# A two-layer hybrid network on one core: both scan directions in one instruction, and attention scores of all keys in one PSUM tile

## The chip, the cores and the metric

The kernel runs on one core of a Trainium2 chip. Each core has a matrix engine (TensorE, PE in the profile, with its weight loads as PEld), three elementwise engines (VectorE = DVE, ScalarE = ACT, GpSimd = POOL), a sync engine that issues the DMAs (SP), and DMA queues. Every engine works through its own instructions in order and waits for the others by semaphores. Matmul results land in PSUM, which has eight banks of 512 F32 columns in 128 partitions each. The metric is device time in microseconds (us); the kernel before takes 4089.88 us, the median of three runs.

## The reference, cut to what matters

Two layers run over 1280 tokens (256 of context, 1024 latent) of width 1024. Layer 0 computes differential attention beside a bidirectional RWKV-7 scan and adds both through one output projection; then comes an MLP. Layer 1 has two other scans and an MLP; the change does not touch it. The two mixers of layer 0:

```python
def _diff_softmax_mix(q, k, v, lam):          # 4 heads, two score maps each
    s = einsum('bhmqd,bhmkd->bhmqk', q, k) * (A_QK_DIM ** -0.5)
    p = softmax(s, axis=-1)
    w = p[:, :, 0] - lam * p[:, :, 1]
    return einsum('bhqk,bhkd->bhqd', w, v)    # then an rmsnorm over each head's 128 columns

def step(S, inp):                             # RWKV-7, 8 heads of 64, once forward, once backward
    r_t, w_t, k_t, v_t, kk_t, a_t = inp
    sa = einsum('bhvk,bhk->bhv', S, kk_t)
    S = (S * w_t - sa * (kk_t * a_t) + v_t * k_t)
    return S, einsum('bhvk,bhk->bhv', S, r_t)
# y = y_forward + flip(y_backward), then a group norm, a bonus term and a gate
```

Context queries see the 256 context keys; latent queries see all 1280.

## The kernel before, in words

Features lie on the partitions and tokens along the free axis, so one tile is 128 features by 1280 tokens. Most matrix products are written as three fp32r matmuls over a high and a low half of each operand (helper lines L82 to L84 or L945 and L946; the splitting subtractions have line L94 and the casts L90 and L92).

Layer 0 goes through three stages that this change touches.

**Pairs.** For each of the four pairs of RWKV heads, `pair` (from L406) takes the projected r, k, v and makes the decay sums `rw_cs` for both directions (a scan on DVE, L426), kk, kk·a and the new k, and writes them in token order to DRAM: `rw_win` holds four slots of a window of 128 tokens, `rw_cs` the decay sums.

**Projections beside the scan.** `at.by_group` projects q, k, v of the attention, with rope, and stores them to DRAM in halves. While it is emitted, the scan's calls to `pump()` advance it by `RATE[0]` generator steps each (class `Pump`), for the first three sweeps (`FIRST`).

**Attention beside the scan.** The scan has ten sweeps of two windows each, one window per direction. A sweep is `prep` for both directions (`prep_dir`: load the window, exponentials `rE`, `rEi` of the decay sums, products `rkr` on DVE at L543 and L544 and `rbk` on POOL at L547, the 128-by-128 score blocks at L555 with their masks at L559, an inverse of a unit triangular matrix in `inverse`, and `values`) and two chunks of `step`, which carry the state `S` (update at L702 and L703). Each direction has its own instructions and its own bank (`si` or `sj` in the inverse, `ss` in the step). When both directions of a window are done, `post` normalizes and stores it (L754 to L772); that is so after the second sweep and after the last four. The pump now advances `at.heads` by `RATE[1]`: for each head and each pair of query blocks, `scores` makes 128 queries by 1280 keys in three pieces of 256, 512 and 512 columns, each in a bank `mm` (two of them), takes a maximum (L948) and an exponential with its sum (L949) of each piece. `factors` works out what each piece is to be scaled by, `mix` scales and subtracts (L977 on POOL, L978 on DVE), transposes the weights (L987), splits them (`a_wh`, `a_wl`) and multiplies by v in three matmuls per 128 keys into `po`.

When the scan is through, the output projection `wout0` starts on the RWKV outputs `o`, with the banks `sp`, `si`, `sj` (`TAIL_TAGS`); what is left of the attention runs beside it.

Within each engine the order of the program is set by a scheduler from the order in which the code is written, the dependencies and its own estimates of time; so the generator steps and the banks set what stands next to what.

## Time and profile before

| | |
|---|---|
| three runs, us | 4087.19, 4089.88, 4095.32 |
| the profiled execution, us | 4086.29, of which 4084.5 from the first to the last instruction (span) |
| mean granted clock of TensorE | 0.942 of full speed |
| PE busy | 3821.4 us (94%), 31232 matmuls |
| DVE busy | 2121.8 us (52%) |
| ACT, POOL busy | 1237.3 us (30%), 1448.5 us (35%) |
| DMA | 392.40 MB, mean 96 GB/s |

Busy time is the union of an engine's instructions. For PE the ends of matmuls are modelled, so neighbouring records overlap, and a slower granted clock makes the same work count as more busy time. Shares over the whole span hide the stages. Those that the change touches lie at 60 to 388 us (pairs), 388 to 742 us (projections beside the scan) and 742 to 1425 us (attention beside the scan), and the end of the attention reaches to about 1500 us. A row of a group view has the line, engine, operation and tiles, then busy time and the mean of one, then how long the engine was idle before them and what released it.

### The profile page before, as it was taken

The numbers are of one execution on the slowest core, as the hardware profiler recorded it, in microseconds if no ns is written. First come the engines' busy times: TensorE is split into PE (matmuls) and PEld (weight loads), VectorE is DVE, ScalarE is ACT, GpSimd is POOL, SyncE is SP. The second block draws the span as 40 slices with busy tenths as digits, with TensorE's granted clock in tenths as the row PEclk, the third lists the DMA queues.
The fourth block names the chain that finished last, engine by engine and source line by source line (L and its number), as shares of the span: only waits on it lengthen the run. The fifth ranks groups of instructions, "written<-read, shape, count | busy, mean of one in ns | idle before, by whom it ended". The sixth has DMA issues, their size and how long they took to land. (4 is left out here: it accounts for less than half of the span.)

```text
span 4084.5 us, 75847 instructions
## 1 busy us (share of the span) xinstructions
PE 3821.4 (94%) x31232; PEld 3137.6 (77%) x31232; DVE 2121.8 (52%) x4634; ACT 1237.3 (30%) x2391; POOL 1448.5 (35%) x1386
## 2 busy tenths in 40 slices
PE   6998899889888799999999999899999889999998
PEld 4765777667666587778878888778876678999897
DVE  6233566777776666333333445447336664443445
ACT  3332323343443425111111112574633141111112
POOL 2321666323433235222122223216524353233323
PEclk9998899888887799999999999999999789999999
DMA  8356654322232522221121102122343311111111
GB/s 306 123 157 191 216 182 161 116 73 90 84 94 57 176 98 90 88 82 64 61 83 52 37 31 89 57 66 81 109 119 104 104 50 57 42 42 58 47 42 63
DMA packets 281882, 392.40 MB, mean 96 GB/s; under 512 B 54080, under 2 KB 184128, under 8 KB 278976
## 3 DMA queue, kind: packets, MB, share of 16 engines
q1 hardware_dynamic: 281536, 387.55, 29.4%
q8 instruction: 246, 4.03, 0.4%
q14 instruction: 100, 0.82, 0.1%
HBM read 295.97 MB, written 91.49 MB: 95 GB/s over the span
## 5 line engine op out<-in xcount | busy, mean ns | idle before, releaser
L82 PE MATMUL mm<-acth,whi 128*128 128x512 f32 (+1 forms) x2376 | 838.4, 354 | 15.0 <-ACT cv_t L1042 7.7
L83 PE MATMUL mm<-actl,whi 128*128 128x512 f32 (+1 forms) x2376 | 834.2, 352 | 18.3 <-DVE actl L255 11.6
L94 POOL TENSOR_TENSOR wlo<-wraw,whi 128x1024 fp32r<-128x1024 f32 (+2 forms) x267 | 557.6, 2094 | 798.1 <-ACT whi L90 795.1
L84 PE MATMUL mm<-acth,wlo 128*128 128x512 f32 (+1 forms) x2376 | 824.7, 351 | 0.0
L82 PEld LDWEIGHTS mm<-acth,whi 128*128 128x128 f32 x2376 | 455.0, 192 | 100.2 <-issue 21.1
L83 PEld LDWEIGHTS mm<-actl,whi 128*128 128x128 f32 x2376 | 455.1, 192 | 87.2 <-DVE actl L255 13.1
L84 PEld LDWEIGHTS mm<-acth,wlo 128*128 128x128 f32 x2376 | 453.4, 192 | 65.7 <-issue 8.0
L90 ACT CAST whi<-wraw 128x1024 fp32r<-128x1024 f32 (+2 forms) x267 | 242.7, 921 | 647.9 <-PE mm L83 265.6
L313 POOL TENSOR_TENSOR relu<-relu 128x256 f32<-128x256 f32 (+1 forms) x192 | 159.9, 833 | 733.3 <-ACT relu L312 731.5
L312 ACT ACTIVATE relu<-mm 128x256 f32<-128x256 f32 (+1 forms) x192 | 93.8, 489 | 819.2 <-PE mm L84 646.6
L92 DVE CAST hidh<-relu 128x256 fp32r<-128x256 f32 (+1 forms) x192 | 71.6, 373 | 450.0 <-POOL relu L313 447.8
L82 PE MATMUL sp<-hidh,whi 128*128 128x256 f32 (+1 forms) x768 | 260.6, 339 | 0.0
L83 PE MATMUL sp<-hidl,whi 128*128 128x256 f32 (+1 forms) x768 | 259.7, 338 | 0.0
L84 PE MATMUL sp<-hidh,wlo 128*128 128x256 f32 (+1 forms) x768 | 259.0, 337 | 0.0
L83 PE MATMUL ss<-hidl,whi 128*128 128x256 f32 (+1 forms) x720 | 242.3, 337 | 1.4 <-DVE hidl L94 1.4
L82 PE MATMUL ss<-hidh,whi 128*128 128x256 f32 (+1 forms) x720 | 242.5, 337 | 0.0
L84 PE MATMUL ss<-hidh,wlo 128*128 128x256 f32 (+1 forms) x720 | 241.9, 336 | 0.0
L337 DVE SCALAR_TENSOR_TENSOR x<-sp,g,x 128x512 f32<-128x512 f32 (+1 forms) x192 | 126.9, 661 | 151.9 <-PE sp L84 151.9
L337 DVE SCALAR_TENSOR_TENSOR x<-ss,g,x 128x256 f32<-128x256 f32 x180 | 119.1, 662 | 148.1 <-PE ss L84 148.1
L949 ACT ACTIVATE a_e<-mm,a_mx 128x512 f32<-128x512 f32 (+1 forms) x208 | 125.7, 605 | 178.6 <-DVE a_mx L948 170.3
L337 DVE SCALAR_TENSOR_TENSOR x<-sp,g2b,x 128x256 f32<-128x256 f32 (+1 forms) x192 | 109.5, 571 | 99.8 <-PE sp L84 98.6
L84 PEld LDWEIGHTS sp<-hidh,wlo 128*128 128x128 f32 x768 | 144.5, 188 | 20.3 <-issue 4.5
(538 smaller groups left out, 7955.6 us busy)
## 6 DMA issues: line engine op xcount, KB each, us to landing
mraw<-in_modw_dram SPq DMA_DIRECT2D x192, 256.0 KB, 3.0
wraw<-in_win_dram SPq DMA_DIRECT2D x75, 512.0 KB, 3.7
wraw<-in_wa_dram SPq DMA_DIRECT2D x64, 512.0 KB, 3.3
wraw<-in_wb_dram SPq DMA_DIRECT2D x64, 512.0 KB, 3.3
rx<-rw_win SPq DMA_DIRECT2D x20, 1024.0 KB, 6.2
x<-in_xT_dram SPq DMA_DIRECT2D x16, 640.0 KB, 8.1
hg<-h SPq DMA_DIRECT2D x32, 256.0 KB, 5.1
wraw<-in_wout_dram SPq DMA_DIRECT2D x32, 256.0 KB, 2.8
```

The source lines that it names most:

```text
L82: self.nc.tensor.matmul(out, lh, rh, start=start and i == 0, stop=False)
L83: self.nc.tensor.matmul(out, lh, rl, start=False, stop=False)
L84: self.nc.tensor.matmul(out, ll, rh, start=False, stop=stop and i == n - 1)
L90: nc.scalar.copy(out=hi, in_=src)
L92: nc.vector.tensor_copy(out=hi, in_=src)
L94: e.tensor_tensor(out=lo, in0=src, in1=hi.bitcast(F32), op=ALU.subtract)
L312: nc.scalar.activation(out=r, in_=ps, func=AF.Relu)
L313: nc.gpsimd.tensor_tensor(out=r, in0=r, in1=r, op=ALU.mult)
L337: nc.vector.scalar_tensor_tensor(out=xg, in0=ps, scalar=gate[:, m, j : j + 1], in1=xg, op0=ALU.mult, op1=ALU.add)
L949: nc.scalar.activation(out=e[:, k0 : k0 + kn], in_=ps, func=AF.Exp, bias=mx, accum_out=o["z"][:, b, m, g : g + 1])
```

## The change

Four things change, and the scheduler moves the rest.

1. `pair` multiplies the decays in once for all tokens, at the end, on tiles of 1280 columns, and writes `rw_kr` and `rw_bk` in the order in which the scan of each direction meets them; `prep` loads them as they are. `rE`, `rEi`, `rkr` and `rbk` of the sweep are gone, and the end-of-chunk decays stay in a constant tile `rw_end`.
2. Both directions go through one instruction per phase: tiles of 16 units in place of 8 in the inverse, 512 columns in place of 256 in `step`. All of the scan, and `post`, takes its PSUM from one tag `rw` with three banks.
3. `scores` puts all keys of 128 queries into one tile `at` of three banks (there is one such tile), with one maximum and one exponential over 1280 columns. The factors between pieces go, and 1/z moves to the norm at the end.
4. The weights and v stay whole F32: one F32 matmul (two passes) in place of three fp32r ones; neither is split. The pump goes at 3.7 and 0.95 steps, and the first-stage projections take turns on `mm` and `po`, one bank each.

```diff
-        wv = lambda slot, lo, hi: self.win[:, lo:hi, slot, i, :].rearrange("w p t -> p w t")
-        nc.sync.dma_start(out=wv(0, 0, P), in_=sv(kk, 0, P))
...
+            nc.scalar.activation(out=E[:, :, 1:65], in_=chunks(cs), func=AF.Exp, scale=-self.HC)
+            nc.gpsimd.tensor_copy(out=self.end[:, :, 4 * d + i : 4 * d + i + 1], in_=E[:, :, 64:65])
+            nc.scalar.activation(out=cs, in_=cs, func=AF.Exp, scale=self.HC)
+            Ei = chunks(cs)
+            for src, e, eng, to in ((kk, E[:, :, 0:64], nc.vector, 0), (kka, Ei, nc.gpsimd, (0, 1)),
+                                    (r, E[:, :, 1:65], nc.vector, 1), (kf, Ei, nc.gpsimd, (1, 0))):
+                t = tmp("rw_t")
+                for a, b in segs:
+                    c = slice(a // 64, b // 64)
+                    eng.tensor_tensor(out=chunks(t)[:, c], in0=chunks(way(src[:, a:b])), in1=e[:, c], op=ALU.mult)
+                if eng is nc.vector:
+                    nc.sync.dma_start(out=self.kr[d][:, :, to, i].rearrange("w p t -> p w t"), in_=t.rearrange("p (w t) -> p w t", t=P))
+                    continue
+                for rows, slot in zip((slice(0, 64), slice(64, P)), to):
+                    nc.sync.dma_start(out=self.bk[d][rows, i, :, slot], in_=chunks(t)[rows])
...
-        return [self.prep_dir(sw, d) for d in range(2)]
...
+        for d in range(2):
+            for c in range(2):
+                tok = slice(c * 64, c * 64 + 64)
+                ps = [n.psum(512, "rw") for _ in range(2)]
+                for i in range(4):
+                    for hh in range(2):
+                        rows = slice(64 * hh, 64 * hh + 64)
+                        nc.tensor.matmul(ps[hh][:, i * P : i * P + P], bk[d][rows, i, c], kr[d][rows, :, i, tok], start=True, stop=True)
+                sc[d, c] = []
+                for hh in range(2):
+                    s = T([P, 4, P], f"rs{hh}", 6)
+                    nc.vector.tensor_tensor(out=s, in0=ps[hh].rearrange("p (i t) -> p i t", i=4),
+                                            in1=k["scmask"].unsqueeze(1).to_broadcast([P, 4, P]), op=ALU.mult)
...
+        o["u"] = self.inverse(mb.rearrange("p d c i t -> p (d c i) t"), sc)
...
+        units = [(d, i, hh, rows) for d in range(2) for i in range(4) for hh, rows in enumerate((A, B))]
+        ps = n.psum(512, "rw")
+        for d, i, hh, rows in units:
+            nc.tensor.matmul(part(ps, d, i)[rows], kr[d][rows, 0, i, tok], S[rows, d, i], start=True, stop=True)
...
-            for (w, y), tag in zip(self.done, ("si", "sj")):
-                self.post(self.out, w, y, tag)
+            for w, d, y in self.done:
+                self.post(self.out, w, d, y, "rw")
...
-        for g, (k0, kn) in enumerate(o["groups"]):
-            ps = n.psum(kn)
...
+        ps = n.psum(1536, "at")
+        qh, ql = o["q"][m]
+        for k0 in range(0, nk, 512):
+            s = slice(k0, min(k0 + 512, nk))
+            nc.tensor.matmul(ps[:, s], qh[:, q], K[m][:, s], start=True, stop=False)
+            nc.tensor.matmul(ps[:, s], ql[:, q], K[m][:, s], start=False, stop=True)
+        mx = o["mx"][:, b, m : m + 1]
+        nc.vector.tensor_reduce(out=mx, in_=ps[:, :nk], op=ALU.max, axis=AX.X, negate=True)
+        nc.scalar.activation(out=e[:, :nk], in_=ps[:, :nk], func=AF.Exp, bias=mx, accum_out=o["z"][:, b, m : m + 1])
...
-                nc.gpsimd.tensor_scalar(out=e1[:, s], in0=e1[:, s], scalar1=f[:, b, 1, g : g + 1], scalar2=1.0, op0=ALU.mult, op1=ALU.mult)
+            nc.vector.scalar_tensor_tensor(out=e0, in0=e1, scalar=f[:, b : b + 1], in1=e0, op0=ALU.mult, op1=ALU.add)
...
-            wh, wl = tl("a_wh", F32R, 512, 2), tl("a_wl", F32R, 512, 2)
-            n.split(wh, wl, ps, "a", "v")
+            w = tl("a_w", F32, 512, 2)
+            nc.scalar.copy(out=w, in_=ps)
+            for kk in range(2):
+                nc.tensor.matmul(po, v[:, 2 * k2 + kk], w[:, kk * 256 : kk * 256 + 256], start=k2 + kk == 0, stop=kk == 1 and k2 == nk // 256 - 1)
...
-TAIL_TAGS = ("sp", "si", "sj")
+TAIL_TAGS = ("rw",)
-FIRST, RATE = 3, (2.6, 1.0)
+FIRST, RATE = 3, (3.7, 0.95)
...
-        n.banks(("mm",), mm=2, po=1, sp=1, si=1, sj=1, ss=2)
+        n.banks(("mm", "po"), mm=1, po=1, at=1, rw=3)
```

How the change moves the instructions is seen at three places. The first is DVE in the attention stage, in the middle of a sweep. Before (`rpm`, `sav`, `S` belong to a step, `rsk`, `rsr`, `id`, `itt` to the next sweep's preparation, `a_` to the attention):

```order
L680 TENSOR_TENSOR rpm<-rbv,ss 128x256
L978 SCALAR_TENSOR_TENSOR a_e_10104<-a_e_10104,a_f,a_e_10194 128x256
L680 TENSOR_TENSOR rpm<-rbv,ss 128x256
L632 COPY_PREDICATED id<-t_masks_85,si 128x16x8
L978 SCALAR_TENSOR_TENSOR a_e_10104<-a_e_10104,a_f,a_e_10194 128x512
L559 TENSOR_TENSOR rsk_12345<-sp,t_masks_85 128x256
L559 TENSOR_TENSOR rsr_12346<-sp,t_masks_85 128x256
L978 SCALAR_TENSOR_TENSOR a_e_10104<-a_e_10104,a_f,a_e_10194 128x512
L619 STREAM_TRANSPOSE itt<-id 128x256
L978 SCALAR_TENSOR_TENSOR a_e_10220<-a_e_10220,a_f,a_e_10246 128x256
L689 TENSOR_SCALAR sav_10128<-ss 64x256
L978 SCALAR_TENSOR_TENSOR a_e_10220<-a_e_10220,a_f,a_e_10246 128x512
```

And the same engine after the change, from a step on:

```order
L667 TENSOR_TENSOR rpm<-rbv,rw 128x512
L925 TENSOR_REDUCE a_mx<-at 128x1
L674 TENSOR_SCALAR sav_7979<-rw 64x512
L683 TENSOR_TENSOR S<-S,rw 128x512
L684 TENSOR_TENSOR S<-S,rw_end 128x512
L925 TENSOR_REDUCE a_mx<-at 128x1
L667 TENSOR_TENSOR rpm<-rbv,rw 128x512
L932 RECIPROCAL a_r<-a_z 128x4
L933 COPY a_rz<-a_r 128x2
L935 SCALAR_TENSOR_TENSOR a_f<-a_r,lam_n,a_z 128x2
L946 SCALAR_TENSOR_TENSOR a_e_9821<-a_e_9935,a_f,a_e_9821 128x1280
L946 SCALAR_TENSOR_TENSOR a_e_10039<-a_e_10088,a_f,a_e_10039 128x1280
```

Before, work of one direction's step lies between pieces of the other direction's preparation and of the attention; after, one step is a run of 512-column instructions, with whole maxima and whole mixes of 1280 columns between its links.

The second place is PE in the same stage. Before (`si` and `sj` are the inverse's banks, `sp` the score blocks, `ss` the step, `mm` and `po` the attention's):

```order
L630 MATMUL si<-id,iwt 32x32 x3
L987 MATMUL mm<-ident,a_e_11022 128x128
L987 MATMUL mm<-ident,a_e_10756 128x128
L987 MATMUL mm<-ident,a_e_11022 128x128
L630 MATMUL si<-id,iwt 32x32 x11
L555 MATMUL sp<-rkr,rbk 128x128 x2
L82 MATMUL po<-a_wh,avh 128x256
L555 MATMUL sp<-rkr,rbk 128x128 x2
L684 MATMUL ss<-rpm,iu 64x64 x11
L83 MATMUL po<-a_wl,avh 128x256
L84 MATMUL po<-a_wh,avl 128x256
```

And after, in the middle of an inverse:

```order
L953 MATMUL mm<-ident,a_e_12039 128x128
L953 MATMUL mm<-ident,a_e_12238 128x128
L618 MATMUL rw<-id,iwt 32x32 x64
L922 MATMUL at<-ak_10905,aqh_12312 128x512
L923 MATMUL at<-ak_10905,aql_12313 128x512
L922 MATMUL at<-ak_10905,aqh_12312 128x512
L923 MATMUL at<-ak_10905,aql_12313 128x512
L922 MATMUL at<-ak_10905,aqh_12312 128x256
L923 MATMUL at<-ak_10905,aql_12313 128x256
L957 MATMUL po<-a_w,av 128x256 x2
```

An inverse's 64 matmuls now stand in one run, followed by the six matmuls of a score tile and two of the weights by v.

The third place is PE where the output projection begins (`o` is the RWKV output, `whi` its weights). Before:

```order
L945 MATMUL mm<-ak_13326,aqh_14849 128x512
L946 MATMUL mm<-ak_13326,aql_14850 128x512
L945 MATMUL mm<-ak_13326,aqh_14849 128x512
L946 MATMUL mm<-ak_13326,aql_14850 128x512
L987 MATMUL mm<-ident,a_e_14390 128x128
L82 MATMUL sp<-o,whi 128x256
L83 MATMUL sp<-o,whi 128x256
L82 MATMUL si<-o,whi 128x512
L83 MATMUL si<-o,whi 128x512
```

After (L690 is the last step's, L734 to L744 the last two posts'):

```order
L690 MATMUL rw<-rs_13596,sav_13428 64x64
L690 MATMUL rw<-rs_13599,sav_13429 64x64
L734 MATMUL rw<-po_y,t_masks_85 128x512
L739 MATMUL rw<-t_masks_85,po_l 128x2 x4
L744 MATMUL rw<-ident,rsy_gn 64x128 x8
L734 MATMUL rw<-po_y,t_masks_85 128x512
L739 MATMUL rw<-t_masks_85,po_l 128x2 x4
L744 MATMUL rw<-ident,rsy_gn 64x128 x8
L82 MATMUL rw<-o,whi 128x256
L83 MATMUL rw<-o,whi 128x256
L82 MATMUL rw<-o,whi 128x512
L83 MATMUL rw<-o,whi 128x512
```

Before, the attention still has rows on PE when the projection starts, and after it; now its last scores and weights stand in front of the inverse of the tenth sweep, only the norm of its last head stands beside that inverse, and from there to the projection PE has nothing but the scan and its posts.

## Rows read from the trace of the kernel before

**Rows 1.** Windows: length, busy us (instructions) by engine, PEclk, DMA share, GB/s

```profile
388.00:742.00 354.00, 317.87 (x4292) 261.63 (x4294) 221.94 (x531) 103.25 (x182) 219.23 (x210) 0.94 0.56 187
742.00:1425.00 683.00, 595.43 (x9209) 465.38 (x9206) 503.18 (x1425) 275.90 (x719) 233.19 (x334) 0.83 0.31 98
1425.00:1510.00 85.00, 81.31 (x451) 68.55 (x451) 60.64 (x111) 25.60 (x63) 23.50 (x30) 0.94 0.21 70
```

**Rows 2.** Timeline: start us, us, engine, line, operation; five marks

```profile
725.15 0.40 PE L84 MATMUL mm<-hg,wlo 128*128 128x512 f32 x1
...
727.93 0.42 DVE L702 TENSOR_TENSOR S<-S,ss 128x256 f32<-128x256 f32 x1
...
1063.57 0.42 DVE L702 TENSOR_TENSOR S<-S,ss 128x256 f32<-128x256 f32 x1
...
1345.99 0.41 DVE L702 TENSOR_TENSOR S<-S,ss 128x256 f32<-128x256 f32 x1
...
1432.37 0.55 PE L82 MATMUL sp<-o,whi 128*128 128x256 f32 x1
```

**Rows 3.** Groups on DVE, 742 to 1425: busy us, mean ns, idle before

```profile
L948 DVE TENSOR_REDUCE a_mx<-mm 128x1 f32<-128x512 f32 x118 | 80.6, 687 | 39.1 <-PE mm L946 38.3
...
L978 DVE SCALAR_TENSOR_TENSOR a_e<-a_e,a_f,a_e 128x512 f32<-128x512 f32 x56 | 54.0, 984 | 0.1
...
L94 DVE TENSOR_TENSOR a_wl<-mm,a_wh 128x512 fp32r<-128x512 f32 x74 | 50.1, 687 | 26.6 <-ACT a_wh L90 26.3
...
L948 DVE TENSOR_REDUCE a_mx<-mm 128x1 f32<-128x256 f32 x76 | 31.7, 421 | 19.6 <-PE mm L946 18.9
...
L559 DVE TENSOR_TENSOR rsk<-sp,t_masks 128x256 f32<-128x256 f32 x51 | 21.4, 419 | 18.4 <-PE sp L555 18.0
...
L543 DVE TENSOR_TENSOR rkr<-rx,rE 128x256 f32<-128x256 f32 x24 | 12.0, 501 | 6.8 <-DMA rx<-rw_win 4.5 <-PE ss L709 2.1
```

**Rows 4.** Waits, same stretch: us in total, times, longest

```profile
ACT a_e L949 <- DVE a_mx L948: 159.3, 123, 8.7
...
PEld mm L945 <- ACT a_e L949: 20.7, 31, 1.6
```

**Rows 5.** Groups on POOL, same stretch

```profile
L977 POOL TENSOR_SCALAR a_e<-a_e,a_f 128x512 f32<-128x512 f32 x56 | 47.4, 858 | 0.0
```

**Rows 6.** Groups on DVE, 60 to 388

```profile
L460 DVE TENSOR_TENSOR rw_kka<-rw_kk,rw_a 128x1280 f32<-128x1280 f32 x3 | 4.5, 1493 | 0.3
```

**Rows 7.** Windows, 60 to 388

```profile
60.00:388.00 328.00, 311.71 (x1680) 227.69 (x1680) 118.24 (x176) 122.10 (x214) 105.59 (x122) 0.93 0.54 168
```

**Rows 8.** Groups on POOL, 60 to 388

```profile
L393 POOL TENSOR_TENSOR f_f_k<-sh_t 128x256 f32<-128x256 f32 x4 | 3.3, 836 | 57.0 <-DMA rw_win<-f_f_k 56.7 <-ACT sh_t L387 0.3
```

**Rows 9.** Groups on ACT, same stretch

```profile
L949 ACT ACTIVATE a_e<-mm,a_mx 128x512 f32<-128x512 f32 x118 | 81.0, 687 | 81.4 <-DVE a_mx L948 81.1
```

**Rows 10.** Timeline on PE: two matmul forms

```profile
1390.90 1.02 PE L756 MATMUL sj<-po_y,t_masks 128*128 128x512 f32 x2
...
1392.11 0.28 PE L83 MATMUL po<-a_wl,avh 128*128 128x256 f32 x1
1392.23 0.28 PE L84 MATMUL po<-a_wh,avl 128*128 128x256 f32 x1
```

**Rows 11.** Timeline on POOL, the last two posts

```profile
1366.97 1.28 POOL L754 TENSOR_TENSOR po_y<-ryt,po_l 128x512 f32<-128x512 f32 x1 [4.49 <-issue]
...
1411.11 1.29 POOL L94 TENSOR_TENSOR po_lo<-po_y,po_hi 128x512 fp32r<-128x512 f32 x1 [2.22 <-DVE po_hi L92]
```

**Rows 12.** Groups on PE, 1425 to 1510

```profile
L82 PE MATMUL si<-o,whi 128*128 128x512 f32 x32 | 13.2, 412 | 0.7 <-DVE x L1681 0.7
...
L84 PE MATMUL sp<-o,wlo 128*128 128x256 f32 x32 | 9.1, 285 | 0.0
...
L987 PE MATMUL mm<-ident,a_e 128*128 128x128 f32 x40 | 7.3, 301 | 2.1 <-DVE a_e L978 2.0
...
L946 PE MATMUL mm<-ak,aql 128*128 128x256 f32 x4 | 1.3, 314 | 0.0
```

More of the change, by code (lines that the diff above doesn't have):

```diff
@@ new lines, in prep, with values @@
+        o = dict(kr=kr, sc=sc, bt=bt, sav=sav)
+        o["u"] = self.inverse(mb.rearrange("p d c i t -> p (d c i) t"), sc)
+        self.values(o)
+        return o
+    def values(self, o):
+        n, nc = self.n, self.nc
+        o["bv"] = self.pool.tile([P, 2, 512], F32, name="rbv", tag="rbv", bufs=2)
+        for c in range(2):
+            ps = n.psum(512, "rw")
+            for d in range(2):
+                sa, sb = o["sc"][d, c]
+                for i in range(4):
+                    cc = slice(i * 64, i * 64 + 64)
+                    oc = slice(d * 256 + i * 64, d * 256 + i * 64 + 64)
+                    nc.tensor.matmul(ps[0:64, oc], sa[64:128, i, 0:64], o["sav"][c][0][64:128, d, cc], start=True, stop=True)
+                    nc.tensor.matmul(ps[64:128, oc], sb[0:64, i, 0:64], o["sav"][c][1][0:64, d, cc], start=True, stop=True)
+            self.pump()
+            nc.scalar.copy(out=o["bv"][:, c], in_=ps)
@@ new lines, in step @@
+        nc.vector.tensor_tensor(out=pm, in0=o["bv"][:, c], in1=ps, op=ALU.add)
+        ps = n.psum(512, "rw")
+        for d, i, hh, rows in units:
+            nc.tensor.matmul(part(ps, d, i)[rows], o["u"][rows, 8 * d + 4 * c + i], part(pm, d, i)[rows], start=True, stop=True)
+        self.pump()
+        flat = lambda t: t.rearrange("p d f -> p (d f)")
+        nc.scalar.activation(out=flat(sav[0][A]), in_=ps[A], func=AF.Copy, scale=-1.0)
+        nc.vector.tensor_scalar(out=flat(sav[1][B]), in0=ps[B], scalar1=-1.0, scalar2=None, op0=ALU.mult)
@@ new lines, in step @@
+        cc = lambda i: slice(i * 64, i * 64 + 64)
+        if not last:
+            ps = n.psum(512, "rw")
+            for d, i, hh, rows in units:
+                nc.tensor.matmul(part(ps, d, i)[rows], o["bt"][d, c][:, i, 64 * hh : 64 * hh + 64], sav[hh][:, d, cc(i)], start=True, stop=True)
+            self.pump()
+            Sn = pool.tile([P, 2, 4, 64], F32, name="S", tag="S", bufs=2)
+            s8 = lambda t: t.rearrange("p d i t -> p (d i) t")
+            nc.vector.tensor_tensor(out=s8(Sn), in0=s8(S), in1=ps.rearrange("p (u t) -> p u t", u=8), op=ALU.add)
+            nc.vector.tensor_tensor(out=s8(Sn), in0=s8(Sn), in1=self.end[:, 2 * sw + c, :].unsqueeze(2).to_broadcast([P, 8, 64]), op=ALU.mult)
+            self.S = Sn
@@ new lines, in step @@
+        ps = n.psum(512, "rw")
+        for q, (d, i, hh, rows) in enumerate(units):
+            nc.tensor.matmul(part(ps, d, i)[rows], S[rows, d, i], kr[d][rows, 1, i, tok], start=q < 2, stop=False)
+        for q, (d, i, hh, rows) in enumerate(units):
+            nc.tensor.matmul(part(ps, d, i)[rows], sav[hh][:, d, cc(i)], o["sc"][d, c][hh][:, i, 64:P], start=False, stop=q >= 14)
+        if c == 0:
+            o["y"] = pool.tile([P, 2, 4, P], F32, name="ryt", tag="ryt", bufs=2)
+        self.pump()
@@ L729, in scan @@
+        nc.scalar.copy(out=o["y"][:, :, :, tok].rearrange("p d i t -> p (d i) t"), in_=ps.rearrange("p (u t) -> p u t", u=8))
+        self.pump()
+        if c == 1:
+            for d in range(2):
+                w, y = self.natural(d, sw), o["y"][:, d]
+                if w in self.half:
+                    self.done.append((w, d, y))
+                else:
+                    self.half.add(w)
+                    nc.sync.dma_start(out=self.yd[w], in_=y)
     def scan(self, pool, pump):
@@ L796, in __init__ @@
         self.q, self.kk = mk("q"), mk("k")
-        self.v = [[d.tile([P, 10, P], F32, name=f"at_v{h}{s}") for s in "hl"] for h in range(4)]
+        self.v = [d.tile([P, 10, P], F32, name=f"at_v{h}") for h in range(4)]
         self.o = d.tile([4, 2, P, NT], F32, name="at_o")
```

343 lines of the change are left out of this document (114 added, 229 removed).

## The prediction, made before the changed kernel ran

> **What bounds the kernel now.** I read the windows first, to find the stage with room. In the attention stage PE is busy 595.4 of 683 us, but at a granted clock of 0.83, between the two levels of 1.2 and 2.4 GHz; in the stage before it is busy 317.9 of 354 us at 0.94, and DVE goes from 63% to 74% busy [rows 1]. So PE carries the load everywhere, with 88 us of gaps in the attention stage and a clock that falls there. What the stage is worth is read from how long a sweep of the scan takes, by the state updates on DVE: the first chunk of the third sweep is at 727.9, of the seventh at 1063.6 and of the last at 1346.0 us [rows 2]. That is 83.9 us a sweep without posts and 94.1 us with them, 88.3 on the mean. The last row of the first-stage projections stands at 725.2, the first of the output projection at 1432.4 [rows 2]. The group rows tell what fills DVE: maxima, mixes, splits of the weights, masks [rows 3]. The waits tell how it goes round: ACT waits 159.3 us for maxima, and PE 20.7 us for exponentials to free a bank [rows 4]. A sweep's 88.3 us hold 65 us of DVE (503.2 times 88.3/683) and 77 us of PE at the low clock. Neither is full: PE stands when a link of the scan, a maximum or an exponential is late, and the stops go with the low clock.
>
> **The change part by part.**
>
> Decays. Sixteen products of 1280 columns and their exponentials enter `pair`. DVE gets eight in all, by the row of a 1280-column product 1.49 us each, so 12 us; POOL eight, by its 858 ns for 512 columns [rows 5] about 2.1 us or, by DVE's neighbour row twice over, 3 us each, so 17 to 24 us [rows 6]. PE is busy 311.7 of those 328 us [rows 7], and DVE and POOL a third, so the work is covered. But POOL already waits 56.7 us in that stage for one tile of k to be written to DRAM before it may be refilled [rows 8], and now k and kk·a are held to the end of the pair. Per pair that is between nothing and 7 us later, −5 to +30 us over all; I take +5, since PE has several tiles of projections to go on with.
>
> First stage. By the order, the projections end 2.25 sweeps into the scan and not 2.85. The 0.6 sweep that is moved behind them is some 33 us of PE per sweep at full clock (my estimate: 77 us at 0.83 is 64, of which the scan has about half), so 20 us at 0.94. The stage also has 36 us of gaps [rows 1]; products `rkr` on DVE (501 ns each, four a sweep and direction [rows 3]) go out of the chain, and v is no longer split. I give that 8 us, between 0 and 20. The projections then end at 725 + 5 − 21 − 8 = 701 us.
>
> Attention on DVE. A full score tile costs 2 x 0.687 + 0.421 = 1.80 us of maxima now; the two rows differ by 0.266 us for 256 columns, so 1280 columns cost 1.49, −20 us for 64 tiles. A mix costs 2.5 times 0.984 = 2.46 us; at 1.5 for 1280 columns, by the product row of the pairs [rows 6], 32 of them give −31. The 84 splits of weights go: −58. The maskings of 256 columns (0.419) become half as many of 512 (0.687 by the split's row): 80 of them, −12. `rkr` goes, 80 at 0.50: −40 [rows 3]. The step's pairs and the inverse's small instructions halve in number; at the 0.155 us that the two maxima rows give for zero columns, some 115 and 220 fewer make −50. Together about −210 of the 786 us of DVE in the three windows, 27%. POOL loses its scalings (858 ns [rows 5]). ACT's exponential goes from 687 ns for 512 columns [rows 9] to under 1.7 us for 1280.
>
> Attention on PE. One F32 matmul replaces three fp32r ones per 128 keys. The fp32r ones start 0.12 us apart at 256 columns; an F32 one of 512 columns takes 1.02 us for two passes with its drain, so some 0.43 us for 256 [rows 10]. 168 times 0.08 is +13 us, spread over the stage: 2 us a sweep.
>
> What a sweep costs then. PE's 77 us are the floor as long as the clock stays at 0.83; at the 0.94 of the stage before they are 68, and 70 with the dearer matmuls. Upward nothing in the rows keeps a sweep from staying at 84, since both directions are now one chain with links of 0.69 where they were 0.42 [rows 3], and no second chain fills PE while one link is on DVE. DVE at 65 x 0.73 = 47 us, some 52 with the attention drawn together, no longer stands in the way. Between 70 and 84 I take 79 for a sweep without posts, nearer to what is seen, and 89 with them; 10 us more is the difference seen now. From 701, 0.6 of a sweep brings the third sweep's mark to 748, four of 79 the seventh's to 1064, two of 89 the ninth's to 1242. The last interval has little attention on PE; I take 84 for it, so 1326.
>
> The end. Behind the last mark there come now 86.4 us to the projection: a second chunk, and two posts that follow each other since there is one buffer, 45.4 us from the first's first to the second's last POOL instruction, with attention rows between their links [rows 11]. Bare, a post is bounded by 12 us (its POOL, DVE and ACT work) and the 22.7 it takes now; I take 15.5, nearer to bare since all attention is gone. The 20 us between the second post's last POOL instruction and the projection bound storing and loading from above, nothing from below; I take 8. Seven for the chunk (20.98 lie now between the mark and the first post), 31 and 8 make 46, and the projection starts at 1372, 60 us earlier. It also runs alone: in the window of the attention's end ten PE groups of the attention, from 7.3 to 1.3 us, add up to 41 us of records, and nine of the projection, from 13.2 to 9.1, to 103 [rows 12]. Records overlap, so the attention's part of the 81.3 busy us is 41/144 of them, 23 us, bounded by 15 and 41.
>
> Sum: 60 + 23 = 83 us off the profiled execution's 4086.3 is 4003. That execution lies 3.6 us below the median of the runs, so I forecast **4006 us**. Nothing behind 1500 us changes.
>
> The bank rule. Two banks of scores now cost PE 20.7 us of waits in 683 [rows 4], since one is read while the other fills. There will be one tile for 1280 keys: 1.1 us of matmuls (four of 512 and two of 256 columns), 1.5 of maximum, up to 1.7 of exponential, 4.3 us times 64 tiles, 275 of some 620 us. By that it does not bind, provided that PE has other work in front of the next score matmul. The Trainium skill (Perfetto Trace Analysis, section Matmuls) says that independent matmul groups should rotate through different PSUM banks, so that reading one overlaps the matmuls of the next. No run here shows a score tile that cannot rotate; by the rule alone all 64 readings of 3.2 us would be PE's loss, 205 us and 4211 in all. The trace agrees as far as it goes: with two banks the loss is 20.7 us.
>
> **The rivals.**
>
> 1. The sweep stays as it is (84, 94, and 94 for the last; the end at 66 us). For it: PE's work is the same, and one chain replaces two that filled each other's gaps. Against: a quarter of DVE's work goes. The marks are then 751, 1087, 1275 and 1369, the projection starts at 1435, and only the attention's 23 us less 3 are won: 4069 us.
> 2. Slower: PE waits at its head for the score tile. PE is in order; where a score matmul comes up before the exponential of the tile before has been read out, everything of the scan behind it stands too, up to 1.5 + 1.7 = 3.2 us. The gain of 83 us is used up at 26 of the 64 tiles; if half of them pay 3.2 us, 102 us are lost: 4108 us. For it: the order puts score tiles and scan links alternately, and a 1.5 us maximum or two mixes of 1.5 stand in front of a link on DVE. Against: in the piece shown after an inverse, 64 matmuls and two of weights stand between tiles.
> 3. More is won: without the stops the clock stays at 0.94, a sweep is 70, one with posts 80, the last interval 72, the end 40: 41 + 18 + 12 + 6 = 77 us more, 3929 us. For it: stage one has 0.94 with a fuller DVE on the same scan. Against: the scan's 32-column matmuls and one chain leave PE standing anyway.
>
> **How the numbers follow.** The forecast's case has 0.53, with a range of its own from 3960 to 4055 (sweep 74 to 84, pairs −5 to +30). Rival 1 has 0.18, rival 2 0.15, rival 3 0.14. The range of 8 in 10 goes from 3915 to 4085: all of rival 3 but its edge, all of rival 1, not rival 2. A difference of 0.2%, 8 us, is what a measurement of this kernel can tell from none. Faster by more: 0.53 and 0.14, and 0.14 of rival 1, so 0.81. Within it: 0.05, the rest of rival 1 and rival 2's edge. Slower: 0.14.
>
> **What would show it.** State updates some 79 us apart before the seventh sweep, at a granted clock above 0.83; DVE busy below 65% in that stage; the last post's matmuls some 45 us behind the last state update, with the projection right behind and no attention in it; waits of PE for the exponential that are about as small as now. I am wrong if the sweeps are 90 us apart or more, if the rows that PE waits for are those of the score tile, or if the first scan sweep starts 20 us later because pairs have become longer.

## The result: slower, and the profile after

The changed kernel takes 4197.58 us (median of four runs), the kernel before beside it 4088.53: a ratio of 1.0262 (95% interval 1.0223 to 1.0301). I had forecast 4006. The profiled execution has a span of 4191.4 us where before it had 4084.5.

The marks that answer to [rows 2], with the first projection beside the scan ahead of them (timeline, columns as there):

```profile
495.32 0.58 PE L82 MATMUL po<-hg,whi 128*128 128x256 f32 x1 [12.30 <-ACT rw_s L480]
...
856.70 0.69 DVE L683 TENSOR_TENSOR S<-S,rw 128x512 f32<-128x512 f32 x1 [1.92 <-PE rw L679]
...
1194.28 0.69 DVE L683 TENSOR_TENSOR S<-S,rw 128x512 f32<-128x512 f32 x1 [2.46 <-PE rw L679]
...
1507.50 0.69 DVE L683 TENSOR_TENSOR S<-S,rw 128x512 f32<-128x512 f32 x1 [1.24 <-PE rw L679]
```

The output projection starts at 1569.9 (1432.4 before). The first projection beside the scan stood at 410.2 before. The 107 us are a sum of six stretches, in us:

| stretch | before | after | difference |
|---|---|---|---|
| to the first projection beside the scan (the pairs) | 410.2 | 495.3 | +85 |
| from there to the third sweep's mark | 317.7 | 361.4 | +44 |
| third to seventh mark, no posts | 335.6 | 337.6 | +2 |
| seventh to tenth mark, with posts | 282.4 | 313.2 | +31 |
| tenth mark to the output projection | 86.4 | 62.4 | −24 |
| from there to the end | 2652.1 | 2621.5 | −31 |

The windows of the stages answer to [rows 1] and [rows 7]:

```profile
60.00:388.00 328.00, 282.39 (x1515) 204.09 (x1507) 114.34 (x165) 111.62 (x186) 114.14 (x123) 0.87 0.46 144
388.00:742.00 354.00, 278.62 (x3232) 223.97 (x3232) 155.11 (x230) 100.36 (x152) 186.16 (x133) 0.86 0.59 185
742.00:1425.00 683.00, 557.34 (x9239) 459.30 (x9233) 377.79 (x727) 231.03 (x404) 131.49 (x137) 0.86 0.27 81
```

The load did go: in the last window DVE is busy 378 us in place of 503, over the whole span 1929.4 in place of 2121.8. But PE, too, is busy less in every window, at a lower granted clock in the first two. These are the same stretches of time and not of work, since the pairs now end at 495 us; between the third and the seventh mark, where the work is the same, PE is busy 281.3 of 337 us in place of 295.7 of 336, at a clock of 0.84 both times. It stands. The group rows of the attention stage (DVE, then ACT and PE) answer to [rows 3, 9, 10]:

```profile
L925 DVE TENSOR_REDUCE a_mx<-at 128x1 f32<-128x1280 f32 x64 | 95.3, 1489 | 76.9 <-PE at L923 76.8
L946 DVE SCALAR_TENSOR_TENSOR a_e<-a_e,a_f,a_e 128x1280 f32<-128x1280 f32 x32 | 48.5, 1558 | 0.3
L548 DVE TENSOR_TENSOR rs<-rw,t_masks 128x512 f32<-128x512 f32 x56 | 37.2, 688 | 36.4 <-PE rw L543 36.2
...
L926 ACT ACTIVATE a_e<-at,a_mx 128x1280 f32<-128x1280 f32 x64 | 84.9, 1327 | 88.1 <-DVE a_mx L925 78.9 <-PE mm L953 9.2
...
L957 PE MATMUL po<-a_w,av 128*128 128x256 f32 x320 | 99.0, 436 | 9.6 <-ACT a_w L955 9.6
```

Where the pairs lose their time is read in one place, the windows around 203 us of after:

```profile
180.00:203.00 23.00, 23.00 (x114) 14.83 (x107) 0.16 (x1) 7.22 (x13) 2.20 (x2) 1.00 0.64 183
203.00:240.00 37.00, 17.08 (x67) 5.60 (x65) 16.38 (x17) 14.13 (x21) 23.67 (x22) 0.57 0.78 223
```

and the second of them in before:

```profile
203.00:240.00 37.00, 37.00 (x189) 25.36 (x188) 12.86 (x20) 15.31 (x27) 8.88 (x14) 0.98 0.61 172
```

PE goes from full to 17 of 37 us, and the granted clock from 1.00 to 0.57. The timeline of after at the end of that stretch (start, us, instruction, idle before and its releaser) says what it stood for:

```profile
230.44 3.04 POOL L501 TENSOR_TENSOR rw_t<-f_f_k,rw_cs 128x256 f32<-128x256 f32 x2
...
233.56 2.46 POOL L391 TENSOR_TENSOR f_f_k<-sh_t 128x256 f32<-128x256 f32 x2
...
236.51 1.33 ACT L385 COPY sh_t<-mm 128x256 f32<-128x256 f32 x3
...
239.04 1.65 PE L162 MATMUL si<-mraw,silu_c 128*32 128x256 f32 x8 [9.87 <-DMA mraw<-in_modw_dram]
240.62 0.58 PE L82 MATMUL mm<-acth,whi 128*128 128x256 f32 x1
```

Read backwards: the next pair's v projection (240.6) needs a free `mm` bank; all three hold r's projection, whose groups ACT copies to `sh_t` only at 236.5, since `sh_t` (one tile) still holds the next k; that k can go to `f_f_k` only at 233.6, since this pair's k is read by the last product from 230.4 on. Before, the same tile was refilled at 189.4. A second held tile ends at almost the same time: ACT waited until 233.7 for the store of one of the four turning tiles (`rw_a` at L416 waits 5.56 us for the DMA `rw_kr<-rw_t`), and was at work on `rw_a` until it could turn to `sh_t`.

### The profile page after: what moved, and what is told of

Its sections match the earlier page's. It is cut to its first block, busy times and chain, and to the rows that moved or that the text cites. A ratio compares the mean times of both kernels' runs of the same rounds, so it can differ in the third digit from the quotient of the medians.

```text
span 4191.4 us, 73710 instructions
## 1 busy us (share of the span) xinstructions
PE 3758.5 (90%) x31064; PEld 3096.2 (74%) x31064; DVE 1929.4 (46%) x3683; ACT 1177.3 (28%) x2011; POOL 1340.5 (32%) x1130
## 2 busy tenths in 40 slices
DMA packets 318219, 387.02 MB, mean 92 GB/s; under 512 B 95040, under 2 KB 224576, under 8 KB 317888
## 4 chain that ended last, share of the span: by engine, by line
PE 68%; DVE 7%; ACT 2%; DMA 2%; issue 2%; POOL 1%; SPq 0%; POOLq 0%; ACTq 0%; DVEq 0%
PE mm L82 9%; PE mm L84 9%; PE mm L83 9%; PE ss L82 4%; PE ss L83 4%; PE ss L84 3%; PE sp L82 3%; PE sp L83 3%; PE sp L84 3%; PE po L957 2%; PE rw L543 1%; PE at L922 1%; DVE a_mx L925 1%; PE si L162 1%; ACT a_e L926 1%
## 5 line engine op out<-in xcount | busy, mean ns | idle before, releaser
L90 ACT CAST whi<-wraw 128x1024 fp32r<-128x1024 f32 (+2 forms) x267 | 242.1, 919 | 706.8 <-PE mm L83 239.4
L312 ACT ACTIVATE relu<-mm 128x256 f32<-128x256 f32 (+1 forms) x192 | 93.8, 489 | 827.0 <-PE mm L84 658.2
L83 PE MATMUL ss<-hidl,whi 128*128 128x256 f32 (+1 forms) x720 | 242.3, 337 | 0.8 <-DVE hidl L94 0.8
L922 PE MATMUL at<-ak,aqh 128*128 128x512 f32 (+1 forms) x208 | 94.6, 455 | 71.5 <-ACT a_e L926 56.7
L82 PEld LDWEIGHTS sp<-hidh,whi 128*128 128x128 f32 x768 | 144.5, 188 | 18.3 <-issue 4.5
```

Source lines behind the costliest of these rows:

```text
L82: self.nc.tensor.matmul(out, lh, rh, start=start and i == 0, stop=False)
L83: self.nc.tensor.matmul(out, lh, rl, start=False, stop=False)
L90: nc.scalar.copy(out=hi, in_=src)
L312: nc.scalar.activation(out=r, in_=ps, func=AF.Relu)
L922: nc.tensor.matmul(ps[:, s], qh[:, q], K[m][:, s], start=True, stop=False)
```

## The experiments

The experiments are single runs, but for e15 and e18. Runs of one kernel differ by up to 28 us (after: 4181.16 to 4209.58; before beside them: 4070.6 to 4093.2), so the marks decide and not the totals. The marks scatter too: in e2, e5, e6, e7, e10 and e13, whose edits leave the scan and the attention alone, a sweep without posts takes 83 to 87 us and one with them 105 to 116 (84.4 and 104.4 after). A pair's length is the distance of the marks "final k" (`f_f_k<-rw_a`): 101.2, 98.7, 93.6 us after, 70.4, 72.1, 72.7 before.

**e1: the decays multiplied in each sweep again, pairs as before.**
```diff
+        nc.sync.dma_start(out=wv(0, 0, P), in_=sv(kk, 0, P))
...
+                        nc.vector.tensor_tensor(out=kr[d][:, q, :, to], in0=x[:, :, back(c)], in1=E[:, :, c, q : q + 64], op=ALU.mult)
```


> Decays are multiplied in every sweep again, as before the change, from the old windows; scan, posts and attention stay as changed. If the pairs' longer ends are what the change lost first, the first projection matmul is back at about 410 us (495 with the change, 410 before) and the time falls by 75 to 95 us, to about 4100 to 4120 us. If the products in the sweep had been what filled DVE and POOL there, sweeps without posts get longer by 5 us or more than the 84 us of the changed kernel and a third of that is given back; if the scan is bound by its chain, they stay at 84.

The projections start at 411.0: the +85 us are the new pairs. But it takes 4181.75, where 4100 to 4120 was expected, as the first stage is 26 us longer and the sweeps are 90 us without posts and 117 with them (84 and 104 after). The multiplication costs about as much in the fused chain.

**e2, e10: the decay sums ahead of the products; at the pair's start.** **e3: packets of 5 KB.** **e5: stores issued from ACT's queue.** **e6: modulation emitted behind the pairs.**
```diff
+            sums.append(cs)
+        for d, cs in enumerate(sums):
```


> In each pair the tanh and the decay sums of both directions come first and the products after them. Theory A (the second direction's chain stands behind the first one's writes, because all its tiles share four buffers, and ACT in order holds up the projections' evictions): a pair is 8 to 20 us shorter than the 102 us of the changed kernel, the first projection matmul comes at 435 to 470 us. Theory B (the many small packets of the writes): no change, 490 to 500 us.

```diff
+            nc.sync.dma_start(out=self.csd[d, i], in_=cs)
```


> The changed kernel with the decay sums at the start of a pair again, parked in DRAM and loaded back at its end, where only exponentials, products and stores are left. Theory R: the chain at the end loses tanh, POOL and the sums, some 7 us a direction; a pair is 82 to 94 us (102), the first projection matmul at 435 to 475 us. Rival W: within 10 us of 495.

```diff
-                    nc.sync.dma_start(out=self.bk[d][rows, i, :, slot], in_=chunks(t)[rows])
+                    nc.sync.dma_start(out=self.bk[d][rows, i, slot].rearrange("p c t -> p (c t)"), in_=t[rows])
```


> The key-side products are written to DRAM with 5 KB in a row in place of 256 B, and read per sweep in twice as many DMAs. Theory B (small packets keep the buffers): the first projection matmul comes at 430 to 460 us and the DMA share of 1.0 at the end of a pair falls below 0.6. Theory A (order and buffers alone): within 10 us of 495.

```diff
-                    nc.sync.dma_start(out=self.bk[d][rows, i, :, slot], in_=chunks(t)[rows])
+                    nc.scalar.dma_start(out=self.bk[d][rows, i, :, slot], in_=chunks(t)[rows])
```


> The stores of the decayed products in a pair are issued by ScalarE's DMA queue and no longer by SyncE's. Theory Q (these stores wait at the head of SyncE's in-order queue until the products are done, and the loads of the modulation weights behind them come late for TensorE): TensorE's waits for those loads in the pairs fall from 37 us to under 15, a pair from 102 to 80 to 92 us, the first projection matmul from 495 to 440 to 475 us. Theory S (the four shared buffers and ScalarE's order hold the pair): within 10 us of 495, or later since ScalarE now waits for products.

```diff
-                    next(mods), next(mods)
```


> The loads and matmuls of the modulation vectors are taken out of the loop over pairs and written behind it. Theory Q: pairs are 70 to 90 us apart (102 with the change). Theory S: 92 to 102 us, less only by the matmuls that were moved. The time as a whole is no test, since the moved loads come in one piece.

All five leave the pairs as they are: the projections start at 491.0, 497.0, 497.8, 503.6 and 499.3 us (4226.38, 4238.21, 4210.59, 4224.46, 4237.08 in all). Order, packets and queue are not the cause (e3 has 23680 packets under 512 B up to the first projection, from 60 us on, in place of 56200). With the stores on ACT's queue PE's waits for `mraw` fall from 35 to 21 us and the pair is as long, so that wait is what PE does while it stands, not why. e6 tells little: the scheduler moved the modulation back between the pairs.

**e7: the second direction's products written into their own tiles.**
```diff
-                t = tmp("rw_t")
+                t = tmp("rw_t") if d else src
```


> The backward direction's products are made first, into the shared buffers, and the forward ones last, in place in kk, r, kk·a and k, so that the next pair's first activation finds a free buffer. Theory S: ScalarE's wait before that activation goes, a pair is 85 to 93 us, the first projection matmul at 450 to 475 us. Theory Q: 95 to 102 us a pair, 480 to 500.

Pairs of 111 and 105 us, start at 519.4, 4242.31: now k's tile is held until its store has landed (POOL waits 21.2 us for the DMA `rw_bk<-f_f_k` before it refills it), and the pair is longer still. That turned the search to who holds a tile.

**e9: the kernel before, its decay sums at the end of the pair.** The two loops over w2 move behind v's stores.


> The kernel before with one edit: the decay sums of both directions are computed at the end of each pair and not at its start; no products, windows as before. Theory R (a chain of both directions' decays at the end of a pair stands on ScalarE's queue in front of the evictions of the next pair's projection, and TensorE runs out of banks): a pair is 78 to 90 us (71 before, 102 with the change), the first projection matmul at 435 to 470 us. Rival W (the products and their stores are what lengthens a pair, wherever the sums stand): 69 to 74 us, 405 to 420 us.

Pairs of 72.7, 70.9 and 72.6 us (4080.36, 4070.60 beside it). The place of the sums costs nothing; what is new in the pairs is only the products with the tiles they hold.

**e13: two tiles for k and for r.**
```diff
-        f = pool.tile([P, NT], F32, name=f"f_{tag}", tag=tag, bufs=1)
+        f = pool.tile([P, NT], F32, name=f"f_{tag}", tag=tag, bufs=2 if tag in ("f_k", "f_r") else 1)
+            n.nw = (2, 2)
```


> The kernel after, with two buffers for the shifted k and r in the pairs (room from the weights: two raw and two split tiles in place of three). Theory H: a pair is long because the one tile of k (and of r) is read by the last products, so the next k and r cannot be written, the evictions and with them the next projections stand. Then the marks of the final k come 75 to 85 us apart in place of 98 to 101, and the projections beside the scan start at 420 to 450 us in place of 495; of the 45 to 75 us, some is given back in the sweeps, as where the old pairs were put back, so 4140 to 4190 in all. Rival X: it is the load of the products and stores themselves; then the marks stay 95 us or more apart, the start at 480 or later, and the time at 4190 to 4240, with fewer weight tiles as a possible loss.

Final k in e13 (timeline):
```profile
167.41 1.49 DVE L440 SCALAR_TENSOR_TENSOR f_f_k<-rw_a,f_f_k 128x1280 f32<-128x1280 f32 x1
262.62 1.49 DVE L440 SCALAR_TENSOR_TENSOR f_f_k<-rw_a,f_f_k 128x1280 f32<-128x1280 f32 x1
354.55 1.49 DVE L440 SCALAR_TENSOR_TENSOR f_f_k<-rw_a,f_f_k 128x1280 f32<-128x1280 f32 x1
429.24 1.49 DVE L440 SCALAR_TENSOR_TENSOR f_f_k<-rw_a,f_f_k 128x1280 f32<-128x1280 f32 x1
```
95.2, 91.9 and 74.7 us; the projections start at 459.0, 36 us earlier, 4174.45. The stretch in which PE stood (columns as [rows 1]) is nearly full again, at nearly full clock:
```profile
203.00:240.00 37.00, 34.67 (x182) 25.33 (x182) 23.96 (x14) 16.48 (x25) 29.09 (x25) 0.99 0.67 195
```
Holding is a cause, but the first two pairs fall short of what theory H expected (75 to 85).

**e16: beside it, posts on `mm` (as e4), two tiles for kk, and three of the products in their own tiles.**
```diff
+        kk = pool.tile([P, NT], F32, name="rw_kk", tag="rw_kk", bufs=2)
+        for d, (w2, hw0) in ((1, (w2b, "hw0b")), (0, (w2f, "hw0f"))):
+                t = tmp("rw_t") if d or src is kka else src
```


> The run with two tiles for k and r and the posts on mm, and beside it two tiles for kk, and the second direction's products of kk, r and k written into their own tiles, so that three of eight products no longer take one of the four turning tiles. Theory H2 (what is left of the longer pairs is the same thing one tile further: kk and the four turning tiles are held until the last products, which put the next kk, a and its square 11 to 15 us late): the marks come 75 to 83 us apart in all three intervals in place of 96, 91 and 75, the projections start at 420 to 435 us in place of 459, and the time, 4136 with the two earlier repairs, falls to 4100 to 4130. Rival L (what is left is the load: four times as many products and a stage with less PE work at hand): marks stay 88 to 96 in the first two intervals, the start 450 to 465, the time 4125 to 4150.

89.2, 88.9 and 71.5 us; start at 448.8; 4119.91 (4073.88 beside it). So the held tiles are 46 of the 85 us; the other 39 stay open. The length of a pair doesn't say where they lie: in the first two intervals of e16 PE stands only 4 and 3 us, but runs 466 and 485 matmuls there (404 and 401 before). Over all, from the start of the kernel to the first projection beside the scan, PE stands 51 us before, 118 after and 78 in e16, and the same 1992 or 1993 matmuls count as 359, 377 and 371 us of busy time. Of the 85 us, then, 67 are standing and 18 busy time at a lower clock (0.85 in place of 0.93). In e16 most of the standing that is left comes behind the third mark (38 us, 18 before). There the first projection waits 14.8 us for the second direction's tanh at the end of the last pair (`rw_s` at L480; 12.3 in its row of after; before it waited 2.7, for another tile).

**e4: posts on the bank `mm`, not on the scan's three.**
```diff
-                self.post(self.out, w, d, y, "rw")
+                self.post(self.out, w, d, y, "mm")
```


> Posts take their PSUM from the transposes' bank in place of the scan's three. Theory P (posts stand in series with the step, because they share the rotation of the scan's banks): from the seventh to the last sweep's first state update takes 265 to 290 us (313 with the change, 282 before) and the time falls by 25 to 45 us. Rival (the post's own work on the engines, or the attention beside it, sets these sweeps): 305 to 320 us and no change of the time beyond 10 us.

From the first projection (495.6) to the third mark (814.7) 319 us, as before, where after has 361; 83.0 us a sweep without posts and 93.8 with them. So the posts on the scan's banks are the whole +44 and +31; e14 and e16, with the same edit, have 321 and 319 us for the first of them. But 4182.42 in all: the waits at its end (columns as [rows 4]) show the last posts late among the attention, and the tenth mark now stands 117 us ahead of the projection.

```profile
POOL po_y L749 <- ACT po_y L748: 101.3, 4, 57.2
ACT a_w L955 <- PE mm L953: 25.2, 9, 4.3
```

**e14: two tiles and posts on `mm` together** (e13's and e4's edits).


> Two buffers for k and r as in the run before, and the posts take the bank mm, not the scan's three. If both repairs add up (pairs 45 to 75 us, of which 10 to 40 stay, posts 15), 4110 to 4170; the posts' share then ends again behind the last sweep, the output projection starting over 100 us after the last state update. Rival: the two shorten stretches that lie beside the same work of the attention, so no more than the better of the two alone, 4150 to 4185.

4136.17: 38 us below e13. The output projection starts at 1508.4, 61 us earlier than after, where e13 alone gives 17 and e4 alone 25; so the two repairs do add up.

**e17: e16 with the posts of the last two sweeps on `rw`.**
```diff
+                self.post(self.out, w, d, y, "mm" if sw < 8 else "rw")
```


> As e16, with the posts of the last two sweeps back on the scan's three banks, those of the earlier ones on mm. If the 117 us between the last state update and the output projection come from posts that wait for the transposes' bank, they become 60 to 85, and the time is 15 to 45 us below e16. If the posts there are late by the attention's DVE and ACT work alone, no change (within 10 us).

4122.69, as e16. The end is 73 us, but the last sweep takes 142 in place of 106: the bank decides only where the last posts' time stands. What would shorten it was not tried.

**e8, e12: the scan without the attention's work, after and before.** Both put zeros in place of the head outputs.
```diff
-                        self.scores(o, kv[0], b, m)
...
+                self.nc.sync.dma_start(out=self.o[hd, half], in_=z)
```


> The attention stage's work is left out (its output is zeros), so that scan and posts run alone after the projections. If a sweep of the changed kernel is set by its own chain (theory C), sweeps without posts stay at 72 us or more (84 with the attention) and those with posts near 100. If the attention sets it (theory T: the one score tile, PE in order), they fall to 50 to 65 us and those with posts to 85 to 95.

> The kernel before without the attention stage's work (its output is zeros). The scan of the changed kernel alone takes 62 us a sweep without posts and 89 with them. If two chains that alternate fill each other's gaps, the one of before takes 50 to 62 us alone and posts add under 12; if fusing shortened the chain, 64 to 75.

Third, seventh and tenth marks of e8 (timeline):
```profile
847.10 0.69 DVE L683 TENSOR_TENSOR S<-S,rw 128x512 f32<-128x512 f32 x1 [1.24 <-PE rw L679]
...
1096.63 0.69 DVE L683 TENSOR_TENSOR S<-S,rw 128x512 f32<-128x512 f32 x1 [3.63 <-PE rw L679]
...
1363.96 0.69 DVE L683 TENSOR_TENSOR S<-S,rw 128x512 f32<-128x512 f32 x1 [1.99 <-PE rw L679]
```

The same marks of e12, of its first direction:

```profile
729.57 0.42 DVE L702 TENSOR_TENSOR S<-S,ss 128x256 f32<-128x256 f32 x1
...
959.53 0.42 DVE L702 TENSOR_TENSOR S<-S,ss 128x256 f32<-128x256 f32 x1 [0.20 <-PE ss L696]
...
1147.40 0.42 DVE L702 TENSOR_TENSOR S<-S,ss 128x256 f32<-128x256 f32 x1
```
Alone, a sweep takes 62.4 us fused and 57.5 in two chains; with posts 89.1 and 62.6. One chain of links of 0.69 us is longer than two of 0.42 side by side, and the two posts of a sweep cost it 27 us where they cost 5. The windows between the third and seventh marks (columns as [rows 1]) and PE's longest row of waits in the first of them (columns as [rows 4]) show how; e8, then e12:

```profile
847.00:1097.00 250.00, 155.56 (x4421) 140.34 (x4422) 93.47 (x217) 32.86 (x56) 37.95 (x56) 0.69 0.19 57
PE rw L612 <- DVE itt L608: 55.9, 8, 12.6
730.00:960.00 230.00, 187.11 (x4553) 163.34 (x4553) 145.28 (x514) 51.21 (x113) 77.89 (x140) 0.72 0.28 96
```
Fused, PE stands 94 of 250 us, 55.9 of them in the inverse, until DVE has transposed a tile for it (`itt`); in two chains it stands 43 of 230, and its longest row of waits is 9.3 us. Three things differ beside the fusing, and none was tried by itself: the scan has three banks in place of five (PE's waits for a reader of one of them, as far as the view shows them, are under 1 us: `rs`, 0.8), the clock is 0.69 in place of 0.72, and only e12 still multiplies the decays in its sweeps, which counts the other way. What the attention adds to a sweep without posts is 22.0 us after (84.4 less 62.4) and 26.4 before (83.9 less 57.5): its gain of 4.4 us is about what the longer chain (4.9) takes. Totals 4048.75 and 3850.91.

**e11: the old form of the attention (pieces in four banks, factors, splits) in the changed kernel.**
```diff
-        ps = n.psum(1536, "at")
+        for g, (k0, kn) in enumerate(o["groups"]):
+            ps = n.psum(kn)
```


> The changed kernel with the attention of before (pieces of at most 512 columns in four rotating banks, factors, split weights), scan and pairs as changed. Theory T (the one three-bank tile and TensorE's order stretch a sweep from 62 us alone to 84): sweeps without posts 70 to 79 us and TensorE's waits for the exponential under a third of the 57 us. Theory D (what stretches it is DVE's and TensorE's plain load of the attention): 84 to 95 us, since DVE gets back its splits and mixes.

88.2 us a sweep and 106.1 with posts, 4218.32. The 2 to 4 us over after are hardly more than the scatter, so this shows that the new form is no loss, and not that it gains. PE's waits of its matmuls for the exponential fall from 56.7 us to 2.8, but those for the mix rise from 11.6 to 40.5, since DVE gets its work back; the score tile's wait alone is not priced by it.

**e15: the kernel before with whole F32 weights and v alone. e18: with two tiles for k and r too.**
```diff
-            wh, wl = tl("a_wh", F32R, 512, 2), tl("a_wl", F32R, 512, 2)
-            n.split(wh, wl, ps, "a", "v")
+            w = tl("a_w", F32, 512, 2)
+            nc.scalar.copy(out=w, in_=ps)
```


> The kernel before with the fourth part of the change alone: the attention's weights and v stay whole F32, one matmul in place of three and no splitting on DVE. Theory D (the splittings on DVE, 58 us of records in the attention stage, lie in the chain of the sweeps): two chains still fill each other's gaps, so a sweep becomes 2 to 6 us shorter: 4040 to 4075, ratio 0.988 to 0.997. Theory N (PE sets the sweep there, and a whole F32 matmul costs as much as the three): no change, 4080 to 4095. Theory S: the F32 matmul is the dearer one on PE, 4095 to 4120.

> The kernel before with whole F32 weights and v (the one part of the change that gained: ratio 0.9981) and two tiles for the shifted k and r. In the pairs of before POOL already waits 43 to 57 us for k's tile, and ACT behind it 28 us. Theory T (a held tile costs only what PE then stands): PE is busy 309 of the 328 us there, so at most some 10 us can come out; pairs 69 to 72 us apart, 4055 to 4075, ratio 0.994 to 0.998. Rival U (each us of that wait counts): pairs 60 to 66 us apart, 4020 to 4050, ratio 0.984 to 0.992.

e15: 4072.77, ratio 0.9981 (0.9969 to 0.9992). Its sweeps without posts take 85.5 us (83.9 before), so the splits on DVE were not what a sweep waited for, against theory D. e18: 4057.29, ratio 0.9933 (0.9919 to 0.9947), the best of all, ahead of both kernels. But its pairs are 70.2, 70.6 and 68.3 us, as theory T says, and its output projection starts at 1435.9, 13.5 us later than in e15: its span is shorter behind that, where its two tiles touch nothing (from the projection to the end 2627.5 us, 2645.7 in e15). That part differs as much between runs of the changed kernel (2609.9 in e1, 2641.5 in e7), whose edits don't touch it either. What the second tiles did to its order was not tried.

## Why the prediction was wrong

**The pairs, the largest miss: +85 in place of +5** (bounds −5 to +30), and the last of the signs that the prediction named for being wrong. The step itself said that k and kk·a are held to the end of the pair, and then let it be covered, "since PE has several tiles of projections to go on with". It has one or two: k's, r's and v's projections leave through one `sh_t`, so behind a held k tile stand three banks and then PE, and the clock goes down with it (0.57). I priced the wait by the row of the wait [rows 8] and not by what queues behind it; e13 and e16 give 46 us back by more tiles; 39 stay open. The wait of before cost little for the same reason: it ended before PE ran out of work, and e18, without it, has the same pairs.

**First stage: mark at 748, measured 857.** Of the 109 us, 80 are the pairs' (495 for 415) and 28 lie in the stretch behind them, whose two posts alone cost 42 (e4). The step counted attention pieces and put nothing for the posts, which now take the banks of the chain.

**Prices of the attention and the scan were right.** Maximum 1.489 us (1.49 forecast), mix 1.558 (1.5), mask 0.688 (0.687), exponential 1.327 (under 1.7). An F32 matmul has two records in the trace, called passes ahead; at full clock they start 0.216 us apart, so it takes 0.43 (0.43; the 436 ns of the row above are the mean of one record). DVE lost 192 us over the span, where 210 less and 12 more in the pairs were forecast. Those 12 were too few: the product of r for the second direction takes DVE 0.96 + 3.37 us and not 1.49, and POOL's products take 2.9 to 4.2 (2.1 to 3).

**Sweeps: 79 and 89 forecast, 84.4 and 104.4 measured.** The step "nothing in the rows keeps a sweep from staying at 84" was the true half. DVE's load was not what a sweep waited for (e15); the chain is longer when fused (e8, e12), and that eats the gain. The attention's own part is a gain of 4.4 us a sweep (e8 and e12). With posts the miss is 15 us a sweep, of which e4 gives 10.6 back: `post` takes three of its tiles in turn from the same three banks as the chain.

**The end: 46 forecast, 62.4 measured; −23 for the attention, measured −31.** Right in sign. The end is bare, as forecast: without any attention it takes 62.6 us (e8). The two posts, on POOL from 1515.5 to 1551.1, follow each other as forecast (31, measured 36). Mis-sized is the term of 8 us for storing and loading: 19 us pass until the weights of the projection have been loaded, cast and split:

```profile
1515.45 1.26 POOL L732 TENSOR_TENSOR po_y<-ryt,po_l 128x512 f32<-128x512 f32 x1 [8.57 <-issue]
...
1549.81 1.26 POOL L94 TENSOR_TENSOR po_lo<-po_y,po_hi 128x512 fp32r<-128x512 f32 x1 [0.54 <-DVE po_hi L92]
1569.94 0.73 POOL L94 TENSOR_TENSOR wlo<-wraw,whi 128x256 fp32r<-128x256 f32 x1 [18.87 <-ACT whi L90]
```
The loads of `o` go out at 1564.4, after a wait of 10.4 us for the store of `po_lo`, and those of the weights behind them at 1566.4. How much of the −31 is the attention's stays open: with no attention at all, e12 is 17.5 us shorter than before in that part (2634.6 us), and the 13 us more lie within the scatter of that part (see e18).

**The rivals.** Rival 2, the slower one (4108), had its mechanism: PE does wait more for the score tile's exponential in the attention stage (66.9 us on the weight loads, against the 20.7 of [rows 4]):

```profile
PEld at L922 <- ACT a_e L926: 66.9, 36, 5.5
PE at L922 <- ACT a_e L926: 56.7, 33, 5.1
```

Yet it isn't the cause of the slowdown: sweeps without posts are as long as before (+2 us in four), and with the old form of the scores, in four banks (e11), they are no shorter. The bank rule that stood behind this rival (the Trainium skill, Perfetto Trace Analysis, section Matmuls: rotate independent matmul groups through different banks) sees the wait, 57 us and not the 205 that the prediction worked out by it; what these 57 are worth by themselves no run shows. Rival 1 had the sweeps without posts right (84), not those with them (94, measured 104.4). For rival 3 the clock would have had to be 0.94; it was 0.84 from the third to the seventh mark. For the slowdown I had no rival with the pairs or the posts in it.

## What to carry to other kernels

Before a read of a single-buffered tile is moved later, follow its producer backwards until an engine stands: tile, eviction, bank, matmul. The wait of one engine is no price; what counts is how many steps of work the last engine in that row still has. A PSUM tag shared between a critical chain and work that only has to be done some time puts both in one line, and giving that work another bank may only move it to the end. And two chains merged into one for fewer instructions lose the overlap of the two: here the scan alone went from 57.5 to 62.4 us a sweep, though DVE had less to do.

## What I had not expected

While PE had little but the modulation's small matmuls, with gaps of up to 10 us (203 to 240 us), its granted clock fell to 0.57, where it was 1.00 in the 23 full us before. From 208.2 to 242.1 it is 0.50, the lower level of 1.2 GHz, and from 242.3 on 1.00 again; so only the first 1.6 us of the projections behind the stall ran at the lower level, and the stall itself is most of what it cost. And writing `rw_bk` in pieces of 5 KB in place of 256 B (e3) shortened neither the pairs nor the stage behind them by more than 10 us, at DMA shares of 0.46 to 0.59; the short packets only pass to the loads (95360 under 512 B on its profile page, 95040 on that of after).
